# Output-weight low parts on the Vector engine, and one weight load moved behind the loads of b22

## The chip, the cores and the metric

The kernel runs on one core of a Trainium2 chip. Its engines work in parallel, each through its own queue in order: TensorE (PE in the profile; its weight loads are PEld), the Vector engine (DVE), the Scalar engine (ACT), GpSimd (POOL), and SyncE (SP), which here only issues DMA transfers. A wait at the head of a queue holds up everything behind it on that engine. The metric is the device time of one execution in microseconds; lower is better.

## What is computed

One layer of an encoder block on x (1, 1024, 1024) in float32, cut to what matters here:

```python
h = layer_norm(x, ln_in_g, ln_in_b)
proj = h @ w_in[l]
att = dilated_attention(aq, ak, av, slopes)
rec = hgrn2(hq, hf_fwd, hf_bwd, hi, hg, lower_bounds[:, l], hgrn_norm_g[l])
merged = sigmoid(ga) * (att @ w_att_up[l]) + sigmoid(gh) * (rec @ w_hgrn_up[l])
h = layer_norm(DEEPNORM_ALPHA * h + merged @ w_o[l], ln1_g[l], ln1_b[l])
gate, up = split(h @ w_ffn_in[l], 2, axis=-1)
h = layer_norm(DEEPNORM_ALPHA * h + (silu(gate) * up) @ w_ffn_out[l], ln2_g[l], ln2_b[l])
```

The change touches the line with `w_o` and the opening of the line with `w_ffn_in`. `w_ffn_in` is (1024, 5632); gate and up are 2816 columns each, worked on in 22 blocks of 128.

## The kernel before

**Precision.** Every matmul operand is split into a high part (a cast to float32r, on ACT, L205) and a low part (source minus high part, L209). `split` puts the low part on POOL unless `eng_lo="dve"` is given. A product is three matmuls per 128 rows: high by high (L255), low by high and high by low (L256, L257, in the order of the operands).

**Phase 2, output product.** The merged activations are transposed in `m0` and `m1`. `wo` has two halves of 512 columns, each a high and a low tile of 128 x 8 x 512. A half is made from four chunks of 128 columns by `wo_chunk`: a 512 KB load on SP into one of two `wraw` buffers (L1164), a cast on ACT and a subtraction on POOL, each over 1024 elements per partition. Chunks 0 to 3 are made during the recurrence's up-projection; chunks 4 to 7 after the pools of that stage are closed, since the second half lies in their memory. The order of TensorE then is: token block 0 with half 0, token block 1 with half 0, token block 0 with half 1, and from there both halves in turn. `half` evacuates a PSUM bank on DVE (L1263); `rest` takes statistics, normalises, transposes (L285) and hands the blocks for the feed-forward on.

**The feed-forward's opening.** The feed-forward input product is a Winograd form: seven products of half-size blocks per f (a pair of gate and up blocks of 128 columns). Their right-hand sides are b11, b21, t1, t2, which stay in SBUF, and b22, t3, t4, which `h1_blocks` stores to the scratch tensors `td[0]`, `td[1]`, `td[2]` (L1308) and `ffn_in` loads again in two pieces each as `t_raw` (L1465), with the high part on ACT and the low part on DVE. `ffn_raws` loads the two weight blocks of an f as `f_raw`, 512 KB each (L1403). The groups for f = 0, 1, 2 are begun early, with their products 1 and 2; then come products 5 and 6 (t1, t2), then 3 and 7 (b22, t3), then 4 (t4). The loads for f = 3 are the first that `ffn_in`'s own loop asks for; each takes the buffer of f = 0.

**What sets the order.** The program is written in one order; a planner then orders each engine's instructions by readiness and priority in a simulated timeline. `add_manual_dep` with a NoSync class adds an edge to that order without a semaphore. `ordered` chains instructions by such edges; `behind` ties one instruction to the last evacuation noted by `left`.

Of the kernel before, what the change touches and what calls it, by code (L numbers as in the profile page):

```python
# [79 lines left out]
class Block:  # L80
# [143 lines left out]
    def left(self, ins):  # L224
        self.gone = ins.ins.name

    def behind(self, ins):

        if self.gone is not None:
            self.tc.add_manual_dep(ins.ins, self.gone, mybir.DependencyInfo(  # L230
                mybir.DependencyClass.NoSync, mybir.DependencyReason.DATA), reason="order behind an evacuation")

    def queued(self, dst, src):
# [923 lines left out]
        for z in (resp, xpool, wspool, blkpool):  # L1157
            z.__exit__(None, None, None)

    def wo_chunk(self, hl, c):  # L1160
        nc, wp = self.nc, self.wp
        hi, lo = hl
        raw = self.wraw.tile([128, KT, 128], F32, name="w_raw", tag="wraw", bufs=2)
        nc.sync.dma_start(raw, self.wo[:, 128 * c:128 * c + 128].rearrange("(k p) c -> p k c", p=128))  # L1164
        s = slice(128 * (c % 4), 128 * (c % 4) + 128)
        self.split(hi[:, :, s], lo[:, :, s], raw)

    def phase2(self):
        nc = self.nc
        gc, bc = self.col["g1"], self.col["b1"]  # L1170
        with ExitStack() as es:
# [31 lines left out]
            wo = [[mp.tile([128, KT, HALF], F32R, name=f"wo0{n}") for n in ("hi", "lo")]]  # L1203
# [17 lines left out]
            wop = es.enter_context(self.pool("wop"))  # L1221
            wo.append([wop.tile([128, KT, HALF], F32R, name=f"wo1{n}") for n in ("hi", "lo")])
            for c in range(4, 8):
                self.wo_chunk(wo[1], c)
            yp = es.enter_context(self.pool("yp"))
            raws = []

# [13 lines left out]
            for t in range(8):  # L1241
                ms = []
                for k0 in (0, 4):
                    mh, ml = self.granules()
                    tk = slice(128 * (t % 4), 128 * (t % 4) + 128)
                    if t < 4:
                        for k in (0, 2):
                            self.split(mh[:, k:k + 2, :], ml[:, k:k + 2, :], m0[(k0 + k) // 2][:, :, tk],
                                       eng_lo="dve" if t == 0 and k0 else "pool")
# [146 lines left out]
        yield  # L1396
        out(1, 0, product(4, 1, False), None)

    def ffn_raws(self, f, pool=None, tag="fraw", bufs=4):
        out = []  # L1400
        for c in (128 * f, D_FF + 128 * f):
            r = (pool or self.rawp).tile([128, KT, 128], F32, name="f_raw", tag=tag, bufs=bufs)
            self.nc.sync.dma_start(r, self.wfi[:, c:c + 128].rearrange("(k p) c -> p k c", p=128))  # L1403
            out.append(r)
        return out

    def ffn_in(self):

        nc = self.nc
        with ExitStack() as es:  # L1410
# [9 lines left out]
            def evac_of(f):  # L1420
                c = acts[f] = fp.tile([128, T], F32, name="fc", tag="fc", bufs=4)
                th = fp.tile([128, T], F32, name="fth", tag="fth", bufs=2)

                def evac(i, l, ps, add):
                    s = slice(HALF * l, HALF * (l + 1))
                    if i == 0:
                        nc.vector.tensor_add(c[:, s], add, ps)
                        nc.scalar.activation(th[:, s], c[:, s], AF.Tanh, scale=0.5)
                        nc.vector.scalar_tensor_tensor(th[:, s], th[:, s], 1.0, c[:, s], op0=OP.add, op1=OP.mult)
                        return  # L1430
                    u = ps
                    if add is not None:
                        u = add
                        nc.vector.tensor_add(u, u, ps)
                    nc.vector.scalar_tensor_tensor(c[:, s], th[:, s], 0.5, u, op0=OP.mult, op1=OP.mult)

                    if l == 0 or f % 2:
                        nc.sync.dma_start(self.gd[4 if l else 1 + f % 2][:, f // 2], c[:, s])

                return evac  # L1440

            def sums(f):

                a11, a21, a12, a22 = (acts[f - 1 + i][:, HALF * l:HALF * (l + 1)] for i in range(2) for l in range(2))
                t = fp.tile([128, T], F32, name="fs", tag="fgl", bufs=2)
                s4 = fp.tile([128, T], F32, name="fs4", tag="fgh", bufs=2)[:, 0:HALF]
                s1, s2 = (t[:, HALF * i:HALF * (i + 1)] for i in range(2))
                nc.vector.tensor_add(s1, a21, a22)
                nc.vector.tensor_sub(a21, a11, a21)
                nc.vector.tensor_sub(s2, s1, a11)  # L1450
                nc.vector.tensor_sub(s4, a12, s2)
                for p, z in ((5, s1), (6, s2), (7, a21), (3, s4)):
                    nc.sync.dma_start(self.gd[p][:, f // 2], z)

            def vecs(v):
                t = self.abp.tile([128, D], F32, name="ab", tag="ab", bufs=2)
                nc.scalar.dma_start(t, bass.AP(tensor=v.tensor, offset=v.offset, ap=[[0, 128], [1, D]]))
                ab.append(t)

            self.first_evac = [evac_of(f) for f in range(3)]  # L1460
            for i, n in enumerate(("b22", "t3", "t4")):
                for k in (0, 2):
                    tag = "fgh" if k else "fgl"
                    r = fp.tile([128, 2, HALF], F32, name="t_raw", tag=tag, bufs=2)
                    nc.sync.dma_start(r, self.td[i][:, k:k + 2, :])  # L1465
                    hi, lo = self.xb[n]
                    self.split(hi[:, k:k + 2, :], lo[:, k:k + 2, :], r, eng_lo="dve")
            ab = []
# [4 lines left out]
            for f in range(2, NF):  # L1473
                if f > 2:
                    grp = self.wino_project(nxt, evac_of(f))
                next(grp)
                if f + 1 < NF:
                    nxt = self.ffn_raws(f + 1)
                next(held, None)
                if f % 2 == 0:  # L1480
                    sums(f - 1)
                next(grp)
                held = grp
                if f == 3:
                    for v in self.ln["1"]:
                        vecs(v)
                if 5 <= f < 21 and f % 2:
                    t = f // 2 - 2
                    n = fp.tile([128, D], F32, name="res", tag="fc", bufs=4)
                    nc.sync.dma_start(n, self.n1_d[t])  # L1490
                    nc.vector.scalar_tensor_tensor(n, n, ALPHA, ab[0], op0=OP.mult, op1=OP.mult)
                    nc.vector.scalar_tensor_tensor(n, ab[1], ALPHA, n, op0=OP.mult, op1=OP.add)
                    nc.scalar.dma_start(self.ahs_d[t], n)
            self.first_rows = []
            for f in range(6):
                p, tag, n = (self.rawp, "fraw", 4) if f < 4 else (self.abp, "ab", 2)
                r = p.tile([128, D], F32, name="w_rows", tag=tag, bufs=n)
# [239 lines left out]
```

## Time and profile before

| | us |
|---|---|
| median of 3 runs | 2134.19 |
| lowest and highest run | 2123.66, 2137.27 |
| profiled execution | 2131.49 |
| its span, first to last instruction | 2129.7 |

| engine | busy us in the profiled execution |
|---|---|
| TensorE matmul | 2029.0 |
| DVE | 1392.7 |
| POOL | 1077.5 |
| ACT | 919.7 |

A row of the timeline has start, length, engine, line, operation, output and inputs, shapes and count; in brackets stands the idle time of that engine before the row and what ended it. A row of the waits view has the waiting instruction, what released it, the total in us, the number of waits and the longest. SPq is SP's queue of DMA issues; its rows span from the first issue to the last of a run of equal ones.

### The profile page before, as it was taken

The numbers are of one execution on the slowest core, as the hardware profiler recorded it, in microseconds if no ns is written. First come the engines' busy times: TensorE is split into PE (matmuls) and PEld (weight loads), VectorE is DVE, ScalarE is ACT, GpSimd is POOL, SyncE is SP. The second block draws the span as 40 slices with busy tenths as digits, with TensorE's granted clock in tenths as the row PEclk, the third lists the DMA queues.
The fourth block names the chain that finished last, engine by engine and source line by source line (L and its number), as shares of the span: only waits on it lengthen the run. The fifth ranks groups of instructions, "written<-read, shape, count | busy, mean of one in ns | idle before, by whom it ended". The sixth has DMA issues, their size and how long they took to land.

```text
span 2129.7 us, 30900 instructions
## 1 busy us (share of the span) xinstructions
PE 2029.0 (95%) x10941; PEld 1674.6 (79%) x10941; DVE 1392.7 (65%) x2228; ACT 919.7 (43%) x1864; POOL 1077.5 (51%) x882
## 2 busy tenths in 40 slices
PE   4799999999999999999999899999999999999998
PEld 3678787788878788887888688878788888887876
DVE  7667746777459753788536712337867677767778
ACT  6544455434544435543355432135433333343542
POOL 3466653567536664465644754443656566630012
PEclk9899999999999999999999999999999999999999
DMA  5342442435424343333444755244434344348423
GB/s 202 109 133 95 147 155 73 144 118 167 130 92 141 135 146 125 124 129 109 146 130 142 283 188 164 89 139 139 154 109 153 129 144 134 117 160 291 158 89 124
DMA packets 273885, 301.10 MB, mean 141 GB/s; under 512 B 14081, under 2 KB 205378, under 8 KB 273730
## 3 DMA queue, kind: packets, MB, share of 16 engines
q1 hardware_dynamic: 266272, 273.73, 39.7%
q10 hardware_dynamic: 7458, 25.40, 3.0%
q8 instruction: 86, 1.41, 0.3%
q14 instruction: 69, 0.57, 0.1%
HBM read 200.25 MB, written 98.83 MB: 140 GB/s over the span
## 4 chain that ended last, share of the span: by engine, by line
PE 77%; DVE 12%; issue 5%; POOL 3%; DMA 2%; ACT 2%; SPq 0%; ACTq 0%; DVEq 0%; POOLq 0%
PE pj L255 17%; PE pj L256 17%; PE pj L257 16%; PE sd L256 6%; PE sd L255 6%; PE sd L257 6%; PE sd L1049 2%; POOL w_lo L209 1%; DVE qd L964 1%; DVE qd L967 1%; PE sd L998 1%; DVE p L849 1%; PE sd L863 1%; DVE fb L953 1%; ACT p L827 1%
## 5 line engine op out<-in xcount | busy, mean ns | idle before, releaser
L209 POOL TENSOR_TENSOR w_lo<-wa,w_hi 128x512 fp32r<-128x512 f32 x276 | 377.4, 1374 | 297.9 <-ACT w_hi L205 274.0
L205 ACT CAST w_hi<-wa 128x512 fp32r<-128x512 f32 x276 | 170.4, 619 | 245.8 <-PE pj L256 159.5
L209 POOL TENSOR_TENSOR w_lo<-wsum,w_hi 128x512 fp32r<-128x512 f32 x88 | 129.0, 1474 | 113.0 <-PE sd L257 60.4
L200 POOL TENSOR_TENSOR mv<-mv,mhalf 128x1 f32<-128x1 f32 x24 | 15.5, 647 | 228.6 <-DVE mv L199 225.5
L209 POOL TENSOR_TENSOR w_lo<-f_raw,w_hi 128x512 fp32r<-128x512 f32 x66 | 102.1, 1555 | 55.4 <-ACT w_hi L205 54.2
L255 PE MATMUL pj<-xt1hi,w_hi 128*128 128x512 f32 x260 | 103.9, 400 | 16.3 <-ACT xt1hi L205 10.7
L205 ACT CAST w_hi<-wsum 128x512 fp32r<-128x512 f32 x88 | 54.7, 621 | 124.6 <-PE sd L256 114.4
L255 PE MATMUL pj<-xb22hi,w_hi 128*128 128x512 f32 x260 | 102.6, 394 | 1.1 <-ACT wkeep L511 1.1
L256 PE MATMUL pj<-xt1lo,w_hi 128*128 128x512 f32 x260 | 102.3, 393 | 0.0
L257 PE MATMUL pj<-xt1hi,w_lo 128*128 128x512 f32 x260 | 102.0, 392 | 0.0
L256 PE MATMUL pj<-xb22lo,w_hi 128*128 128x512 f32 x260 | 101.5, 390 | 0.0
L257 PE MATMUL pj<-xb22hi,w_lo 128*128 128x512 f32 x260 | 101.3, 390 | 0.0
L209 POOL TENSOR_TENSOR w_lo<-ws,w_hi 128x512 fp32r<-128x512 f32 x46 | 63.0, 1373 | 69.2 <-ACT w_hi L205 63.3
L205 ACT CAST gwsum<-a_raw 128x512 fp32r<-128x512 f32 (+1 forms) x78 | 47.8, 616 | 102.9 <-PE pj L256 48.0
L511 ACT COPY wkeep<-pj 128x512 f32<-128x512 f32 x138 | 80.1, 582 | 22.1 <-DVE evh L430 10.1
L403 DVE TENSOR_TENSOR evh<-wkeep,pj 128x512 f32<-128x512 f32 x66 | 57.5, 879 | 48.5 <-PE pj L257 35.2
L209 DVE TENSOR_TENSOR gwkeep<-a_raw,gwsum 128x512 fp32r<-128x512 f32 (+1 forms) x78 | 57.7, 739 | 43.1 <-ACT gwsum L205 40.2
L489 POOL TENSOR_TENSOR wa<-wa,wa 128x512 f32<-128x512 f32 x46 | 67.6, 1480 | 35.6 <-DVE ws L488 27.6
L414 DVE TENSOR_TENSOR evh<-wkeep,pj 128x512 f32<-128x512 f32 x48 | 32.6, 681 | 80.7 <-PE pj L257 65.5
L255 PE MATMUL pj<-xt4hi,w_hi 128*128 128x512 f32 x192 | 77.8, 406 | 5.6 <-DVE evh L403 5.6
L257 PE MATMUL pj<-xt2hi,w_lo 128*128 128x512 f32 x192 | 76.1, 397 | 4.9 <-POOL w_lo L209 4.9
L255 PE MATMUL pj<-xb11hi,w_hi 128*128 128x512 f32 x192 | 77.3, 404 | 2.6 <-DVE evh L414 1.4
(406 smaller groups left out, 6587.1 us busy)
## 6 DMA issues: line engine op xcount, KB each, us to landing
wa<-in_w_in_dram SPq DMA_DIRECT2D x184, 256.0 KB, 3.1
f_raw<-in_w_ffn_in_dram SPq DMA_DIRECT2D x44, 512.0 KB, 4.2
a_raw<-gd SPq DMA_DIRECT2D x30, 512.0 KB, 3.5
gd<-fc SPq DMA_DIRECT2D x44, 256.0 KB, 2.0
gd<-fs SPq DMA_DIRECT2D x33, 256.0 KB, 2.1
tg<-evh SPq DMA_DIRECT2D x32, 256.0 KB, 3.5
tg<-tg SPq DMA_DIRECT2D x16, 512.0 KB, 3.7
y<-ahs SPq DMA_DIRECT2D x16, 512.0 KB, 5.5
```

The costliest lines, as they stand in the source:

```text
L205: nc.scalar.copy(hi, src)
L209: ins = e.tensor_sub(lo, src, hi.bitcast(F32))
L255: nc.tensor.matmul(ps, whi, xhi, start=first, stop=False, **kw)
L256: nc.tensor.matmul(ps, whi, xlo, start=False, stop=False, **kw)
L257: nc.tensor.matmul(ps, wlo, xhi, start=False, stop=last, **kw)
L403: self.left(nc.vector.tensor_tensor(o, self.order_src(add, g, kind), s, OP.add))
L414: self.left(nc.vector.tensor_add(t, add, ps))
L489: nc.gpsimd.tensor_sub(a["a21"], a["a11"], a["a21"])
L511: nc.scalar.copy(t, ps)
L827: nc.scalar.activation(z, z, AF.Exp, bias=N0[p, hd, tt:tt + 1], scale=QSCALE, accum_out=L0[p, hd, tt:tt + 1])
L849: nc.vector.tensor_scalar(z, z, W0[p, hd, tt:tt + 1], None, op0=OP.mult)
L1049: nc.tensor.matmul(po[:, jj, :], l, r, start=(n == 0), stop=(n == len(terms) - 1))
```

## The change

`wo_chunk` gets an argument for the engine of the low part, and chunks 4 to 7 pass "dve". `behind` may be given the instruction to stand behind; `ffn_raws` may pass one on; `ffn_in` keeps the name of the last of b22's two loads, and the loads for f = 3 (made in the loop's step f = 2) are ordered behind it.

```diff
-    def behind(self, ins):
-
-        if self.gone is not None:
-            self.tc.add_manual_dep(ins.ins, self.gone, mybir.DependencyInfo(
+    def behind(self, ins, last=None):
+
+        last = last or self.gone
+        if last is not None:
+            self.tc.add_manual_dep(ins.ins, last, mybir.DependencyInfo(
...
-    def wo_chunk(self, hl, c):
+    def wo_chunk(self, hl, c, by="pool"):
...
-        self.split(hi[:, :, s], lo[:, :, s], raw)
+        self.split(hi[:, :, s], lo[:, :, s], raw, eng_lo=by)
...
             for c in range(4, 8):
-                self.wo_chunk(wo[1], c)
+                self.wo_chunk(wo[1], c, "dve")
...
-    def ffn_raws(self, f, pool=None, tag="fraw", bufs=4):
+    def ffn_raws(self, f, pool=None, tag="fraw", bufs=4, after=None):
...
-            self.nc.sync.dma_start(r, self.wfi[:, c:c + 128].rearrange("(k p) c -> p k c", p=128))
+            ins = self.nc.sync.dma_start(r, self.wfi[:, c:c + 128].rearrange("(k p) c -> p k c", p=128))
+            if after:
+                self.behind(ins, after)
...
-                    nc.sync.dma_start(r, self.td[i][:, k:k + 2, :])
+                    ins = nc.sync.dma_start(r, self.td[i][:, k:k + 2, :])
+                    if i == 0:
+                        b22_load = ins.ins.name
...
-                    nxt = self.ffn_raws(f + 1)
+                    nxt = self.ffn_raws(f + 1, after=b22_load if f == 2 else None)
```

## The prediction, made before the change was run

> **What bounds the kernel now.** I read the page's first part, then the windows view with the span cut into stages, then the waits of TensorE after 1370 us, and last the timeline, engine by engine, around the two places those waits name.
>
> ```profile
> PE 2029.0 (95%) x10941; PEld 1674.6 (79%) x10941; DVE 1392.7 (65%) x2228; ACT 919.7 (43%) x1864; POOL 1077.5 (51%) x882
> ...
> 1376.00:1475.00 99.00, 96.13 (x446) 79.46 (x445) 48.22 (x98) 43.12 (x79) 44.44 (x38) 0.98 0.45 148
> 1475.00:1522.00 47.00, 42.23 (x176) 33.23 (x175) 40.50 (x44) 23.11 (x39) 27.00 (x19) 0.93 0.48 149
> 1522.00:1895.00 373.00, 373.00 (x1647) 308.60 (x1646) 268.75 (x255) 138.08 (x238) 234.27 (x157) 1.00 0.40 134
> ```
>
> The columns of the last three rows are the stretch, its length, then busy time and count of PE, PEld, DVE, ACT and POOL, the granted clock, the DMA share and GB/s. TensorE is the bound: 95% of the span. In the 373 us from 1522 it never stops (373.00 busy, 373 / 1647 = 0.226 us per matmul), so what is won ahead of 1522 is not absorbed there. The changed code lies in the first two stages, which is where TensorE does stop:
>
> ```profile
> PE sd L255 <- ACT xb22hi L205: 4.2, 1, 4.2
> PE pj L256 <- POOL wo1lo L209: 1.7, 1, 1.7
> PE pj L255 <- ACT wo1hi L205: 1.2, 1, 1.2
> ```
>
> The lower two are one place (the second half of the output weights), the upper one the other (b22). Each part of the change aims at one of them.
>
> **First part: low parts of output-weight chunks 4 to 7 on DVE.** What TensorE loses there:
>
> ```profile
> 1386.74 0.39 PE L257 MATMUL pj<-wo0hi,w_lo 128*128 128x512 f32 x1
> 1388.31 0.73 PE L255 MATMUL pj<-wo1hi,w_hi 128*128 128x512 f32 x2 [1.18 <-ACT wo1hi L205]
> 1390.74 0.80 PE L256 MATMUL pj<-wo1lo,w_hi 128*128 128x512 f32 x1 [1.69 <-POOL wo1lo L209]
> ...
> 1393.79 0.39 PE L257 MATMUL pj<-wo1hi,w_lo 128*128 128x512 f32 x1
> ...
> 1390.00:1391.00 1.00, 0.26 (x1) 0.26 (x2) 0.00 (x0) 0.00 (x0) 0.68 (x1) 0.62 1.10 332
> 1393.00:1394.00 1.00, 1.00 (x4) 0.81 (x3) 0.00 (x0) 0.00 (x0) 0.00 (x0) 0.67 0.68 203
> ```
>
> The next matmul was due at 1386.74 + 0.23 = 1386.97. Between it and 1393.79 nine start (two at 1388.31, then seven from 1390.74 on), worth 9 x 0.226 = 2.0 us. The place therefore costs 6.8 - 2.0 = 4.8 us: some 3.4 of waiting and 1.4 of slow clock, since the granted clock falls in 1390 to 1391 (0.62) and is back in 1393 to 1394 (0.67).
>
> The chain behind it:
>
> ```profile
> 1376.74 2.00 ACT L205 CAST wo1hi<-w_raw 128x1024 fp32r<-128x1024 f32 x2
> 1387.21 1.04 ACT L205 CAST wo1hi<-w_raw 128x1024 fp32r<-128x1024 f32 x1 [1.42 <-DMA w_raw<-in_w_o_dram]
> 1378.45 4.75 POOL L209 TENSOR_TENSOR wo1lo<-w_raw,wo1hi 128x1024 fp32r<-128x1024 f32 x2
> 1385.87 4.81 POOL L209 TENSOR_TENSOR wo1lo<-w_raw,wo1hi 128x1024 fp32r<-128x1024 f32 x2 [2.67 <-ACT wo1hi L205]
> 1380.87 2.75 SPq L1164 DMA_DIRECT2D w_raw<-in_w_o_dram  x2
> w_raw<-in_w_o_dram SPq DMA_DIRECT2D x2, 512.0 KB, 3.9
> 1377.01 0.88 DVE L1210 TENSOR_TENSOR mT<-mT,tg 128x512 f32<-128x512 f32 x1
> 1382.45 0.69 DVE L191 BATCH_NORM_STATS2 bn<-y 128x6 f32<-128x512 f32 x1
> 1387.17 0.69 DVE L1263 SCALAR_TENSOR_TENSOR y<-pj,y 128x512 f32<-128x512 f32 x1 [4.02 <-PE pj L257]
> L209 DVE TENSOR_TENSOR xt3lo<-t_raw,xt3hi 128x1024 fp32r<-128x1024 f32 x2 | 2.4, 1210 | 0.0
> ```
>
> There are two raw buffers. Chunks 4 and 5 lie in them; POOL needs 2.4 us for each low part, and only when one is done may SP load chunk 6 (1380.87) and chunk 7 (about 1383.2). A load lands 3.9 us later, ACT takes 1.04, POOL 2.4 again, and TensorE needs all four chunks.
>
> After the change four POOL subtractions of 2.4 us go (9.6 us) and four DVE ones of the same shape come. The row for that shape on DVE with POOL idle is xt3lo: 1.21 each, 4.8 us in all. DVE is free from 1377.01 + 0.88 = 1377.89, so chunk 4 is done at 1379.1, chunk 5 (its high part is ready at 1378.74) at 1380.3. The two loads leave then: 1.8 and 2.9 us earlier. Chunk 7 lands at 1380.3 + 3.9 = 1384.2, or some 1385.2 if it shares the engines with chunk 6 (my allowance). ACT: 1386.2; DVE: 1387.4. The first two matmuls need the high part only, 1386.97 + 2 x 0.226 = 1387.4. So the wait just closes, no clock falls, and the gain is the whole 4.8 us. The cover for the DVE work is its own idle time: 4.02 us before the evacuation at 1387.17. Who waits behind a DVE that stands at chunk 6 or 7 is the evacuation L1263 and its statistics; TensorE takes nothing of them before the transposes of that row block, 19 us later (the chain of waits, start and length), so that costs nothing.
>
> ```profile
> 1406.23 0.87 PE sd L285 x8
> ```
>
> Upper end for the subtraction:
>
> ```profile
> 1511.10 2.30 DVE L209 TENSOR_TENSOR xb22lo<-t_raw,xb22hi 128x1024 fp32r<-128x1024 f32 x1
> 1508.66 3.66 POOL L209 TENSOR_TENSOR w_lo<-wsum,w_hi 128x512 fp32r<-128x512 f32 x2 [3.79 <-ACT w_hi L205]
> ```
>
> This one began while POOL worked until 1508.66 + 3.66 = 1512.32, and took 2.30. I take 1.21, the nearest row, since POOL has nothing left after its activation splits at 1378.45; 2.30 is kept for a rival. The Trainium skill (SBUF — State Buffer, "SBUF: two separate sides") states a rule against this part: a DVE operation with two SBUF inputs and a GpSimd operation that reads SBUF exclude each other, the later one blocks entirely. The trace agrees: 1.22 us to POOL's end plus 1.21 makes 2.43, against 2.30. By it chunk 4 would start at 1378.45 instead of 1377.9 and the sum would be 0.5 us smaller.
>
> **Second part: the weight block behind b22.** What is lost, and the chain:
>
> ```profile
> 1503.49 0.39 PE L257 MATMUL pj<-xt2hi,w_lo 128*128 128x512 f32 x1
> 1508.12 1.31 PE L255 MATMUL sd<-xb22hi,w_hi 128*128 128x512 f32 x2 [4.24 <-ACT xb22hi L205]
> 1509.38 0.79 PE L256 MATMUL sd<-xb22lo,w_hi 128*128 128x512 f32 x1
> ...
> 1513.27 0.40 PE L257 MATMUL sd<-xb22hi,w_lo 128*128 128x512 f32 x1
> ...
> 1492.76 6.82 SPq L1308 DMA_DIRECT2D td<-tsum  x2
> 1499.67 0.58 SPq L1403 DMA_DIRECT2D f_raw<-in_w_ffn_in_dram  x1
> 1500.36 2.26 SPq L1465 DMA_DIRECT2D t_raw<-td  x4
> ...
> 1517.46 8.35 SPq L1403 DMA_DIRECT2D f_raw<-in_w_ffn_in_dram  x2
> ...
> 1507.02 1.04 ACT L205 CAST xb22hi<-t_raw 128x1024 fp32r<-128x1024 f32 x1 [4.71 <-DMA t_raw<-td]
> 1503.66 1.75 DVE L1344 TENSOR_TENSOR wsum<-f_raw 128x512 f32<-128x512 f32 x1
> 1508.09 1.23 DVE L209 TENSOR_TENSOR xb22lo<-t_raw,xb22hi 128x1024 fp32r<-128x1024 f32 x1 [2.68 <-ACT xb22hi L205]
> ```
>
> From 1503.49 + 0.23 = 1503.72 to 1513.27 eleven matmuls start (two at 1508.12, nine from 1509.38 on), worth 2.5 us, and take 9.55: 7.0 lost. On SP stand, in this order: the stores of t3 and t4 (done issuing at 1492.76 + 6.82 = 1499.58), one f_raw load at 1499.67 (the gate block of f = 3), then b22's two loads and t3's two. b22's first load is issued at 1500.36 and lands only at 1507.02, 6.7 us later, behind the 512 KB of the f_raw block. The change puts that f_raw behind b22's second load; the other f_raw block of f = 3 comes at 1517.46 and is behind it either way.
>
> Nothing is added or removed; one issue of 0.6 us and its transfer change place. b22's first load is issued at 1499.67. Its landing time alone: the same shape from the other scratch tensor,
>
> ```profile
> a_raw<-gd SPq DMA_DIRECT2D x30, 512.0 KB, 3.5
> ```
>
> gives 1503.2; with the t4 store still ahead of it I take 1503.7. ACT is done at 1504.8, and TensorE starts its first two matmuls 3.3 us earlier. The low part needs DVE, which is busy until 1503.66 + 1.75 = 1505.41, then takes 1.23. So the shift is capped by DVE: exactly the 2.68 us for which it stood idle before xb22lo. DVE is nearly full in this stage (40.50 of 47 us, those 2.68 among the rest), so the whole opening moves by 2.7 us and no more. Bounds: 0 if t3's loads come late in b22's place (the f_raw block now runs between them), and 4.5 (7.0 less the 1.1 us to 1504.8 and the 1.4 between two high-part matmuls and a low part at 1506.6) if another order of DVE's queue lifts the cap. I take 2.7.
>
> The moved block has no early reader; the first is
>
> ```profile
> 1528.90 1.78 DVE L1344 TENSOR_TENSOR wsum<-wsum,f_raw 128x512 f32<-128x512 f32 x1
> ```
>
> 29 us after its issue, so its delay of a few us costs nothing.
>
> **Sum.** 4.8 + 2.7 = 7.5 us. The profiled execution took 2131.49 us (its span 2129.7 and 1.8 around it): 2124.0. It lies 2.7 below the median of the runs shown (2134.19), so on the median: 2126.7.
>
> **Rivals.**
>
> *Half of the first part.* DVE puts the evacuation at 1387.17 and its statistics (0.69 each) ahead of chunk 7, or the subtractions cost 2.30. Then the last low part is done near 1389.8, only 0.9 ahead of 1390.74: gain 0.9 + 2.7 = 3.6, time 2130.6. For it: chunk 7 and that evacuation fall due within 1 us of each other. Against: DVE has 4 us of idle time there.
>
> *The b22 part gives nothing.* t3 or the t4 store sets the pace of the opening: gain 4.8, time 2129.4. For it: the same 2.5 MB pass the queue. Against: the second f_raw and t4 are not needed until much later. This is also the case in which the change doesn't do what it says, if another load takes the freed place ahead of b22.
>
> *Slower.* The first two low parts stand in DVE's queue behind the first evacuation, which waits for TensorE and ends with its statistics at 1382.45 + 0.69 = 1383.1 (POOL had done one by 1380.8). Then 1384.3 and 1385.5 for them, loads land at 1388.2 and 1390, ACT 1391.0, DVE 1392.3: 1.5 us later than 1390.74, and a second dip of the clock costs 1.4 again. That is +2.9 where -4.8 was expected. It decides as soon as that evacuation is ahead of chunk 4 and the b22 part brings less than 2.9; with that part at 0.4, +2.5: 2136.7. Against it: chunk 4 is ready 3.8 us before the evacuation.
>
> **How the numbers follow.** Forecast 0.50, half of the first part 0.15, b22 nothing 0.17, slower 0.13, something unnamed 0.05. The likeliest case gives 2126.7. Its own range is 2125 to 2129 (second part 4.5 to 0). The runs of before spread from 2123.66 to 2137.27 about 2134.19, so the low end is 2126.7 - 10.5 = 2116; the high end takes in the slower rival, 2138. One per cent is 21 us, about what a measurement of this kernel can tell from no change. No case reaches it; I leave 0.03 to faster and 0.04 to slower by over 1%.
>
> **What would show it.** Right: TensorE's waits on wo1hi and wo1lo gone or under 0.5 us and no dip of the clock near 1390; wo1lo on DVE at 1.2 us; chunk 7 loaded near 1380.3; the f_raw of f = 3 after b22's second load; the wait on xb22hi at 1 to 2 us with DVE's idle time before xb22lo gone. Wrong: a TensorE wait on a DVE wo1lo of 2 us or more, a new wait on xt3hi or xt3lo, or new waits in the 373 us that have none now; the last would mean that the order of the feed-forward's instructions changed as a whole.

## The result, and the profile after

| | before | after |
|---|---|---|
| median of 18 runs each, us | 2131.06 | 2124.05 |
| lowest and highest run | 2122.23, 2137.27 | 2116.25, 2128.63 |
| profiled execution | 2131.49 | 2124.65 |
| its span | 2129.7 | 2122.8 |

The ratio after to before is 0.997, with a 95% interval of 0.9958 to 0.9982: a small gain, but a sure one. TensorE's order of instructions is the same in both kernels. DVE's order has four subtractions more and POOL's four fewer, and on SP the weight block moved. With the weight block the planner also exchanged neighbours in the opening, at two places on DVE (the second xt4lo now stands behind both multiplications of L1432 and directly ahead of wkeep) and at three on ACT; the kernel with the first part alone has none of these exchanges. TensorE's waits of the kernel after, from 1490 to 1525 us, the stretch of the second place (the view has none for the first place, 1370 to 1420):

```profile
PE sd L256 <- ACT xb22hi L205: 1.8, 1, 1.8
PE sd L257 <- DVE xt3lo L209: 0.7, 1, 0.7
PE sd L256 <- DVE wkeep L1437: 0.6, 1, 0.6
PE sd L257 <- DVE xb22lo L209: 0.2, 1, 0.2
```

The two waits on the output weights are gone, and the wait on b22 fell from 4.2 to 1.8 us, but three small new ones stand behind it (xt3lo, wkeep, xb22lo), all on DVE. The windows view of the kernel after, same stretches and columns as in the prediction:

```profile
1376.00:1475.00 99.00, 98.88 (x465) 82.16 (x464) 56.61 (x106) 44.35 (x82) 36.85 (x37) 1.00 0.47 152
1475.00:1522.00 47.00, 43.10 (x185) 33.35 (x184) 42.87 (x45) 23.50 (x39) 30.16 (x19) 1.00 0.47 146
1522.00:1895.00 373.00, 373.00 (x1647) 308.96 (x1646) 266.99 (x256) 138.52 (x238) 229.69 (x154) 1.00 0.40 134
```

The granted clock is 1.00 in the first two stretches (0.98 and 0.93 before): both dips are gone in this execution. The 373 us still have no idle time, so what was won ahead of them was kept.

The first place in the timeline of the kernel after:

```profile
1379.02 2.88 DVE L209 TENSOR_TENSOR wo1lo<-w_raw,wo1hi 128x1024 fp32r<-128x1024 f32 x2
1380.80 1.52 SPq L1165 DMA_DIRECT2D w_raw<-in_w_o_dram  x2
...
1386.54 1.05 ACT L205 CAST wo1hi<-w_raw 128x1024 fp32r<-128x1024 f32 x1 [0.62 <-DMA w_raw<-in_w_o_dram]
...
1387.62 1.23 DVE L209 TENSOR_TENSOR wo1lo<-w_raw,wo1hi 128x1024 fp32r<-128x1024 f32 x1 [0.44 <-ACT wo1hi L205]
...
1388.17 0.61 PE L256 MATMUL pj<-wo1hi,w_hi 128*128 128x512 f32 x2
1388.76 0.68 DVE L1264 SCALAR_TENSOR_TENSOR y<-pj,y 128x512 f32<-128x512 f32 x1
1388.90 0.51 PE L257 MATMUL pj<-wo1lo,w_hi 128*128 128x512 f32 x1
...
1390.64 0.40 PE L258 MATMUL pj<-wo1hi,w_lo 128*128 128x512 f32 x1
```

TensorE comes to the second half at 1388.17 and goes on at 1388.90; nine matmuls start from 1388.17 to before 1390.64, worth 2.04 us of the 2.47, so 0.4 us is lost here where 4.8 was. Chunk 7's low part is done at 1388.85, and the evacuation (L1264) runs behind it.

The second place:

```profile
1496.59 1.95 SPq L1468 DMA_DIRECT2D t_raw<-td  x4
1498.66 3.45 SPq L1404 DMA_DIRECT2D f_raw<-in_w_ffn_in_dram  x2
...
1500.35 0.39 PE L258 MATMUL pj<-xt2hi,w_lo 128*128 128x512 f32 x1
1500.49 1.75 DVE L1345 TENSOR_TENSOR wsum<-f_raw 128x512 f32<-128x512 f32 x1
1501.46 1.04 ACT L205 CAST xb22hi<-t_raw 128x1024 fp32r<-128x1024 f32 x1 [2.32 <-DMA t_raw<-td]
1502.54 1.23 DVE L209 TENSOR_TENSOR xb22lo<-t_raw,xb22hi 128x1024 fp32r<-128x1024 f32 x1 [0.29 <-ACT xb22hi L205]
1502.56 1.02 PE L256 MATMUL sd<-xb22hi,w_hi 128*128 128x512 f32 x2 [1.82 <-ACT xb22hi L205]
1503.82 0.50 PE L257 MATMUL sd<-xb22lo,w_hi 128*128 128x512 f32 x1 [0.24 <-DVE xb22lo L209]
...
1515.20 1.28 DVE L1432 SCALAR_TENSOR_TENSOR fth<-fth,fc 128x512 f32<-128x512 f32 x2
```

The four loads of b22 and t3 now go out ahead of both f_raw blocks. b22 is there 4.9 us after its issue (6.7 before), and DVE's idle time ahead of xb22lo fell from 2.68 to 0.29 us.

The clock had a share in the second place too. The windows of the kernel before:

```profile
1506.00:1507.00 1.00, 0.00 (x0) 0.00 (x0) 0.00 (x0) 0.00 (x0) 0.00 (x0) 0.65 0.97 393
...
1508.00:1509.00 1.00, 0.89 (x2) 0.57 (x2) 0.91 (x1) 1.00 (x4) 0.34 (x1) 0.50 1.01 406
...
1513.00:1514.00 1.00, 1.00 (x6) 0.82 (x5) 1.00 (x2) 0.00 (x0) 0.00 (x0) 0.94 0.10 29
```

A mean of 0.65 is 0.7 us at 0.50, one of 0.94 is 0.1, so the clock was halved from 1506.3 to 1513.1, 6.8 us. Of these, 5.0 lie behind the start of b22's product at 1508.12, and 2.5 of the 7.0 us lost there are theirs. The kernel after has no such dip here.

To compare executions, each profile is cut at four TensorE starts that every kernel has: the first output product, the first matmul of t1 (product 5), and the first matmul that writes pj in t4's product (product 4 of the second f). "Head" is all before the first, "wo" lies between the first two and holds the first place, "opening" between the second and the third and holds the second place, "tail" is the rest of the span. All in us, worked out from the timelines:

```
kernel            span     head      wo      opening   tail
before            2129.7   1376.09   116.02  37.95     599.64
before_again      2131.6   1379.34   116.79  38.06     597.41
after             2122.8   1377.29   111.67  35.54     598.30
after_again       2121.5   1374.64   111.95  36.73     598.18
only_wo           2119.5   1371.65   111.66  38.55     597.64
wo_45             2125.0   1374.42   115.41  38.23     596.94
wo_67             2128.0   1373.53   115.79  38.31     600.37
only_b22          2125.5   1374.69   116.15  36.72     597.94
only_b22_again    2122.6   1371.74   116.23  36.82     597.81
t4_act            2127.2   1376.65   111.82  39.10     599.63
fth_behind        2123.6   1374.72   111.65  40.48     596.75
b22_first         2125.0   1380.86   112.03  34.07     598.04
b22_first_again   2117.4   1373.32   112.38  34.06     597.64
f3_late           2117.7   1373.07   112.14  35.87     596.62
```

In the first pair the 6.9 us of span are 4.35 in wo, 2.41 in the opening and 1.34 in the tail, less 1.20 lost in the head. Every engine's order is the same in all of these kernels up to the end of the head, and yet the head lies anywhere from 1371.7 to 1380.9. The spans of two single executions can therefore not be set against each other at this size; the two stages in which the change lies can, since they repeat far better.

The clock differs in the opening as well. It is halved there for 6.8 us in the five profiles with the loads as before and in `t4_act`, for 3.4 us in `after_again`, both of `only_b22`, `fth_behind` and `f3_late`, and not at all in the first profile of the kernel after and both of `b22_first`.

### The profile page after: what moved, and what is told of

Read it like the earlier page. It is cut to its first block, busy times and chain, and to the rows that moved or that the text cites. A ratio compares the mean times of both kernels' runs of the same rounds, so it can differ in the third digit from the quotient of the medians.

```text
span 2122.8 us, 30900 instructions
## 1 busy us (share of the span) xinstructions
PE 2026.3 (95%) x10941; PEld 1673.6 (79%) x10941; DVE 1399.0 (66%) x2232; ACT 919.5 (43%) x1864; POOL 1068.7 (50%) x878
## 4 chain that ended last, share of the span: by engine, by line
PE 54%; DVE 7%; DMA 2%; issue 2%; POOL 2%; ACT 1%; SPq 0%; ACTq 0%; DVEq 0%; POOLq 0%
PE pj L258 11%; PE pj L257 11%; PE pj L256 11%; PE sd L257 6%; PE sd L256 6%; PE sd L258 6%; POOL w_lo L209 1%; PE sd L1050 1%; ACT p L828 1%; DVE qd L965 1%; PE sd L999 0%; DVE fb L954 0%; DVE wa L494 0%; DVE p L850 0%; DMA binb<-in_ln_in_b_dram 0%
## 5 line engine op out<-in xcount | busy, mean ns | idle before, releaser
L490 POOL TENSOR_TENSOR wa<-wa,wa 128x512 f32<-128x512 f32 x46 | 68.0, 1490 | 36.8 <-DVE ws L489 33.5
L256 PE MATMUL pj<-xt2hi,w_hi 128*128 128x512 f32 x192 | 77.4, 404 | 1.8 <-ACT xt2hi L205 1.8
```

The source lines that it names most:

```text
L256: nc.tensor.matmul(ps, whi, xhi, start=first, stop=False, **kw)
L490: nc.gpsimd.tensor_sub(a["a21"], a["a11"], a["a21"])
```

## The experiments

The labels are those of the table. The kernels of one group ran on one chip, beside the kernel before.

### The two parts apart, and the first part in halves

`only_wo` is the change without its second part, `only_b22` without its first. `wo_45` and `wo_67` take the first part alone, for two of its four chunks.

```diff
 # only_wo, wo_45, wo_67
-                    nxt = self.ffn_raws(f + 1, after=b22_load if f == 2 else None)
+                    nxt = self.ffn_raws(f + 1, after=None)
 # only_b22
-                self.wo_chunk(wo[1], c, "dve")
+                self.wo_chunk(wo[1], c)
 # wo_45
+                self.wo_chunk(wo[1], c, "dve" if c < 6 else "pool")
 # wo_67
+                self.wo_chunk(wo[1], c, "pool" if c < 6 else "dve")
```

> The first part alone (low parts of chunks 4 to 7 on DVE; the weight load of f = 3 stays ahead of b22). Theory: the two parts are separate places with separate prices, so this one gives what the stage with the output weights gave in the changed kernel, 4.4 us: TensorE has no wait on wo1hi or wo1lo over 0.3 us, the clock stays at 1.00 from 1376 to 1400 us, and the later wait on xb22hi stays at 4.2 us with its clock dip. Span about 2125, ratio about 0.998. Rival (the two places share one cost, for instance the phase of the clock window): the gain alone is 2 us or less, or 6 and more.

> The second part alone (low parts stay on POOL; the load of f = 3 behind b22). Theory: 2.4 us, the wait on xb22hi falls from 4.2 to 1.8 us and DVE's idle time before the first xb22lo from 2.68 to about 0.3; the waits on wo1hi (1.2) and wo1lo (1.7) stay, with the clock dip near 1390. Span about 2127, ratio about 0.999. Rival (the wait also gets a full clock back, which DVE does not cap): 4 us.

> Only chunks 4 and 5 have their low parts on DVE, 6 and 7 on POOL; the b22 part is left out. Theory: the gain has two halves, the raw buffers freed sooner (loads of 6 and 7 leave some 1.3 and 2.2 us earlier) and the last subtractions shorter. Here the loads leave early, but POOL then needs 2 x 2.4 us for chunks 6 and 7, so TensorE's wait on wo1lo is still about 2 us: gain 1 to 1.5 us, and up to 1.4 more if the clock does not dip. Rival A (the buffers' release is all): 4.4 us, no wait left. Rival B (the last subtractions are all): 0.

> Only chunks 6 and 7 have their low parts on DVE, 4 and 5 on POOL; the b22 part is left out. Theory: the loads leave as late as before (the second near 1383.2), chunk 7's high part is ready near 1388.2 and its low part 1.2 us later instead of 2.4: the wait on wo1hi stays at 1.2, that on wo1lo falls from 1.7 to about 0.5: gain about 1.2 us, and up to 1.4 more if the clock does not dip. Rival A (the buffers' release is all): 0. Rival B (the last subtractions are all): 4.4 us.

Measured against the kernel before (median 2129.29): `only_wo` 2124.34, ratio 0.9973 (0.9963 to 0.9984); `only_b22` 2128.90, 0.999 (0.9978 to 1.0002); `wo_45` 2127.22, 0.9994 (0.9984 to 1.0005); `wo_67` 2127.73, 0.9993 (0.9983 to 1.0003).

The first part stands alone: wo falls from 116.02 to 111.66, and the opening does not gain (38.55). The second part alone brings 1.2 us in the opening, half of what the first profile of the kernel after showed; its own ratio does not tell it from no change.

The halves bring little: 0.6 and 0.2 us in wo against the first profile of the kernel before, 0.9 and 0.5 against the mean of the four profiles without the first part (116.3). Some 1 to 1.5 us was expected of each, and the waits did shrink about as expected. So neither the earlier release of the buffers nor the shorter last subtractions is the gain by itself. Waits of `wo_67`:

```profile
PE pj L256 <- ACT wo1hi L205: 1.5, 1, 1.5
PE pj L257 <- DVE wo1lo L209: 0.6, 1, 0.6
```

That is 2.1 us against 2.9 before, and `wo_45` waits 2.28. Part of it was handed back by the clock. The windows of `wo_45` around its wait:

```profile
1388.00:1389.00 1.00, 0.79 (x3) 0.70 (x4) 0.00 (x0) 0.00 (x0) 0.16 (x1) 0.91 1.01 303
1389.00:1390.00 1.00, 1.00 (x3) 0.73 (x3) 0.00 (x0) 0.00 (x0) 0.00 (x0) 0.50 0.51 149
1390.00:1391.00 1.00, 1.00 (x4) 0.78 (x3) 0.00 (x0) 0.00 (x0) 0.00 (x0) 0.50 1.00 297
1391.00:1392.00 1.00, 1.00 (x4) 0.81 (x3) 0.00 (x0) 0.00 (x0) 0.00 (x0) 0.50 0.42 120
1392.00:1393.00 1.00, 1.00 (x5) 0.78 (x5) 0.00 (x0) 0.55 (x2) 0.07 (x1) 0.88 0.00 0
```

From 1388.8 to 1392.2 (0.91 and 0.88 are the ends of it) the granted clock is 0.50, and a matmul starts every 0.43 us instead of every 0.23. In the kernel before, part of such a stretch fell into the wait itself (0.26 us of TensorE work in the window from 1390); here the wait is over sooner and the whole stretch runs under load. Counted as in the prediction, `wo_45` loses 4.2 us at the place (13 matmuls start between 1385.31 and 1392.42), some 2.5 by standing and 1.7 by the clock, and `wo_67` the same; before it was 4.8 (3.3 and 1.5). So while the wait only shrinks, the clock keeps its 1.5 and takes 0.2 more. Only a wait that closes takes the dip along: all eight profiles with the whole first part have at most 0.6 us of waiting at the place and no dip near 1390, all six others stand there for 2 us or more and have it.

### Does DVE cap the second part?

The prediction's cap says that b22 may land as early as it likes, since DVE is busy. `t4_act` lets b22 land earlier still: t4's last store, which stands ahead of b22's loads on SP, is issued from ACT. `b22_first` does the same and also lifts the cap: two multiplications of the evacuations of f = 0 and 1 (L1432) are ordered behind b22's second low part on DVE. `f3_late` tests that the moved block has no early reader, and puts it behind t4's last load. `before_again` shows what two profiles of one kernel differ by.

```diff
 # t4_act, b22_first
-            nc.sync.dma_start(self.td[i][:, :, c], v)
+            (nc.scalar if t == 7 and i == 2 else nc.sync).dma_start(self.td[i][:, :, c], v)
 # b22_first (split returns its last instruction)
-                        nc.vector.scalar_tensor_tensor(th[:, s], th[:, s], 1.0, c[:, s], op0=OP.add, op1=OP.mult)
+                        o = nc.vector.scalar_tensor_tensor(th[:, s], th[:, s], 1.0, c[:, s], op0=OP.add, op1=OP.mult)
+                        if f < 2 and l == 0:
+                            self.behind(o, self.b22_low)
...
-                    self.split(hi[:, k:k + 2, :], lo[:, k:k + 2, :], r, eng_lo="dve")
+                    low = self.split(hi[:, k:k + 2, :], lo[:, k:k + 2, :], r, eng_lo="dve")
+                    if i == 0:
+                        self.b22_low = low.ins.name
 # f3_late
-                    if i == 0:
+                    if i == 2:
                         b22_load = ins.ins.name
```

> Both parts, and the last store of t4 (token block 7) leaves on ACT's queue instead of SP's, so that b22's loads no longer stand behind a store that waits for DVE: they can leave some 6 us earlier. TensorE's order is that of the changed kernel, DVE's has one pair swapped. Theory (DVE caps the opening: it is busy without a pause until the first xb22lo): the wait on xb22hi (1.8 us) goes, a wait on xb22lo of about 2 us comes in its place, DVE's idle time before xb22lo (0.29) goes; the opening, from the first matmul with xt1 to the product with xt4 that took 35.54 us in the changed kernel and 37.95 before, is shorter by 0.3 us at most. Rival (the landing of b22 is the cap): shorter by 1.8 to 2.8 us, no wait on b22 left.

> As t4_act, and the two operations of the first evacuations on DVE that stand ahead of xb22lo (2.4 us in the changed kernel) are ordered behind the second xb22lo. Theory (DVE's order caps the opening): xb22lo starts up to 2.4 us earlier and TensorE waits for b22 under 1 us in all; the opening takes 33.5 to 34.5 us, ratio to before about 0.996. Rival (DVE's total work caps it, whatever the order: it is 40 to 43 us of the 47 us stage): the wait moves to xt3lo, xt4lo or wkeep and the opening stays at 35 us or more.

> Both parts, but the loads of f = 3 stand behind the last load of t4 instead of the last of b22, some 5 us later still. Theory: the block is first read by DVE 20 us and more after its issue, so the opening stays at 35.5 us to within 0.5 and there is no wait on f_raw or on s2 (wsum). Rival (the moved block is late for someone): a new wait of DVE on the load of f_raw and an opening longer by 2 us or more.

> The kernel before, unchanged, for a second profile. Theory: of the stretches compared, the one from the first output product to the first matmul with xt1 (116.02 us) and the opening (37.95 us) repeat within 0.5 us, apart from the phase of the clock window, while the 1376 us ahead of them and the 600 us behind them differ by 1 to 4 us from run to run. Rival: all four repeat within 0.5 us, so that the 1.3 us which the changed kernel gained behind the opening belong to the change.

Measured against the kernel before (median 2131.15): `t4_act` 2125.52, ratio 0.9975 (0.9964 to 0.9987); `b22_first` 2122.22, 0.9954 (0.9937 to 0.9971); `f3_late`, one run, 2119.46; `before_again`, one run, 2133.41.

`t4_act`, timeline:

```profile
1498.19 1.06 ACT L205 CAST xb22hi<-t_raw 128x1024 fp32r<-128x1024 f32 x1
1499.47 1.78 DVE L1345 TENSOR_TENSOR wsum<-f_raw 128x512 f32<-128x512 f32 x1
1500.13 0.61 PE L256 MATMUL sd<-xb22hi,w_hi 128*128 128x512 f32 x2
1501.18 1.75 DVE L1432 SCALAR_TENSOR_TENSOR fth<-fth,fc 128x512 f32<-128x512 f32 x1
1502.86 2.29 DVE L209 TENSOR_TENSOR xb22lo<-t_raw,xb22hi 128x1024 fp32r<-128x1024 f32 x1
...
1505.19 0.80 PE L257 MATMUL sd<-xb22lo,w_hi 128*128 128x512 f32 x1 [4.45 <-DVE xb22lo L209]
```

b22's high part is ready before TensorE comes to it, and TensorE does not wait for it at all; then it waits 4.45 us for the low part, because DVE is at other work until 1502.86. The cap holds: the earlier landing moved the wait to DVE and did not shorten the opening. It even lengthened it to 39.10, which was not expected: DVE stood idle 0.96 us before this work, so that xb22lo began 14.4 us after the start of product 5 instead of 13.6 in the kernel after; the subtraction itself took 2.29 us; and the clock was halved for 6.8 us. This execution was the longest of the 12.

`b22_first`, timeline:

```profile
1503.88 2.32 DVE L209 TENSOR_TENSOR xb22lo<-t_raw,xb22hi 128x1024 fp32r<-128x1024 f32 x1
1504.53 0.61 PE L257 MATMUL sd<-xb22hi,w_hi 128*128 128x512 f32 x2
1506.25 0.50 PE L258 MATMUL sd<-xb22lo,w_hi 128*128 128x512 f32 x1 [1.11 <-DVE xb22lo L209]
...
1510.21 1.28 DVE L1433 SCALAR_TENSOR_TENSOR fth<-fth,fc 128x512 f32<-128x512 f32 x2
```

With those multiplications out of the way TensorE waits 1.1 us for the first low part and 0.8 for the second (under 1 in all was expected), and the opening is 34.07, 3.9 shorter than before. DVE's order is not the only difference, though: the planner gave TensorE another order as well. Eight matmuls that write pj with t2 now stand ahead of the first ones with t4, which in the kernel after wait 0.6 us for wkeep and here for nothing. As long as TensorE's order is the same, for the first 86 matmuls of the opening, `b22_first` leads the kernel after by 0.4 us; at the end of the opening it leads by 1.5. How much of that is due to DVE's order and how much to TensorE's no run separates.

`f3_late` has an opening of 35.87, as good as that of the kernel after (35.54): the f = 3 blocks go out 18.8 us after the start of product 5 instead of 9.7, and TensorE waits for nothing of theirs. `before_again` repeats the opening within 0.1, and wo only within 0.8, where 0.5 had been expected; its tail is 2.2 shorter than in the first profile of the same kernel. So the 1.34 us in the tail of the first pair are within the scatter.

### Repeats, and the order of DVE alone

`after_again`, `b22_first_again` and `only_b22_again` are the same kernels once more, to see what of the second part repeats. `fth_behind` is `b22_first` with t4's store back on SP: the order of DVE's queue without the earlier landing.

> The changed kernel once more, beside b22_first on the same chip. Theory: ratio to before 0.997 again; in the profile the stretch from the first output product to xt1 repeats at 111.7 us within 0.3, with no wait over 0.5 us on wo1, and the opening lies between 35 and 37 us, according to how many DVE operations meet a POOL subtraction (0.7 or 1.8 us, 1.2 or 2.3 us for the same operation). Rival: the opening repeats to 0.2 us, and the 36.72 us of only_b22 come from the first part's absence.

> b22_first once more on the same chip as after_again. Theory: the opening is again 1 to 2 us shorter than that of after_again, 34 to 35 us, and the ratio to before some 0.0005 to 0.001 below that of after_again. Rival: the difference was scatter; the same ratio and the same opening within 0.3 us.

> The second part alone once more, one look. Theory: the opening varies with the meetings of DVE and POOL, so it lies anywhere from 35 to 37 us, and the wait on xb22hi is 1.8 to 2.1 us again. Rival: 36.7 us to within 0.2.

> Both parts and only the order of DVE from b22_first (the two operations of the first evacuations behind the second xb22lo), with t4's last store back on SP, so that b22 lands as late as in the changed kernel. Theory: now the landing is the cap; DVE stands idle 2 us and more before xb22lo and does the 2.4 us of work after it, so the opening is no shorter than in the changed kernel, 35.5 to 38 us, with the wait on xb22hi at 1.8 us still there. Rival (the order of DVE alone gives b22_first's gain): 34 us.

Measured against the kernel before (median 2128.54): `after_again` 2122.04, ratio 0.9979 (0.9967 to 0.999); `b22_first_again` 2121.36, 0.9971 (0.9956 to 0.9985); `only_b22_again`, one run, 2124.38; `fth_behind`, one run, 2125.43.

The opening of `b22_first` repeats to 0.01. That of the kernel after doesn't: 36.73 instead of 35.54, and `only_b22` stays at 36.8. So 35.54 was the lucky one. What differs is seen in the waits of `only_b22`,

```profile
PE sd L256 <- ACT xb22hi L205: 1.9, 1, 1.9
...
PE sd L256 <- DVE wkeep L1437: 1.5, 1, 1.5
```

and in the timeline of `after_again`:

```profile
1511.83 3.48 DVE L1432 SCALAR_TENSOR_TENSOR fth<-fth,fc 128x512 f32<-128x512 f32 x2
1515.23 2.31 DVE L209 TENSOR_TENSOR xt4lo<-t_raw,xt4hi 128x1024 fp32r<-128x1024 f32 x1
1517.46 0.68 DVE L1437 TENSOR_TENSOR wkeep<-wkeep,sd 128x512 f32<-128x512 f32 x1
```

The same pair of DVE multiplications took 1.28 us in the first profile and 3.48 here, and both times in `only_b22`. In the first profile POOL had next to nothing to do during them; here it worked all the time. TensorE pays for it with a longer wait on wkeep (1.2 to 1.6 us against 0.6). These three executions also have one dip of the clock in the opening, which the first profile lacks. In `after_again` TensorE comes to that wait 0.6 us later than in the first profile, but DVE, at work without a pause from 1510.05 on, ends it 1.2 us later, and behind it both need the same 5.1 us. So the 1.2 us come by way of DVE; how far the dip had made DVE's own inputs late stays open. `f3_late` has the dip and the slow pair and still reaches 35.87: there the second xt4lo stands ahead of the pair, and TensorE does not wait for wkeep.

`fth_behind` makes the opening worse than was expected (35.5 to 38), 40.48: the wait on xb22hi stays at 1.8, the multiplications now stand in front of t3's low part, and TensorE waits 2.2 us for xt3lo and 2.1 for wkeep. The order pays only together with the earlier landing.

`b22_first` has the shortest opening, 1.5 and 2.7 us shorter than those of the kernel after. That its total is shorter is not shown: beside each other on one chip the two have 0.9971 and 0.9979, and the intervals overlap.

## Why the prediction was right, point by point

**The time.** Predicted 2126.7, measured 2124.05; predicted for the profiled execution 2124.0, measured 2124.65. The predicted change was -7.5; the medians differ by 7.0 and, in the repeat, 6.5. The measured median lies just below the 2125 to 2129 given for the likeliest case, because the median of the kernel before came down with it, from 2134.19 in 3 runs to 2131.06 in 18. That the profiled execution was met within 0.7 us is luck: its head alone ranges over 9 us.

**The first part: mechanism right, the term 0.4 too large.** Predicted -4.8. Over all profiles that hold the whole first part, eight, wo has a mean of 111.9; over the four that hold none of it, 116.3: -4.4. Step by step, with the 1.2 us added by which TensorE was later here: chunk 7's data were predicted for 1386.4 and came at 1386.5, its low part for 1388.6 and came at 1388.85; 0.4 us were lost where none was predicted. The step that was off is the price of the first subtraction. The lines view of the kernel after, with minimum, median and maximum in ns:

```profile
L209 DVE TENSOR_TENSOR wo1lo<-w_raw,wo1hi x4: 1209/1226/1747, 1379.0 to 1387.6; 128x1024 fp32r<-128x1024 f32 x4
```

Three took 1.2 us as predicted, the first 1.75: POOL was still at its activation splits when it began. That repeats: the first took 1.75 us in all nine profiles with chunk 4 on DVE. The prediction had reckoned this way and then set it aside: the Trainium skill (SBUF — State Buffer, "SBUF: two separate sides") has whichever of the two engines comes second blocked for the whole of the other's instruction, which gave 0.5 us less, thus 4.3. The run sides with the Trainium skill: 4.35 in the first pair, 4.4 in the mean. That this half microsecond is all that was missing is likely but not shown, since wo itself repeats only within 0.8.

**The rivals to the first part.** DVE put the first evacuation behind chunks 4 and 5 and the second behind chunk 7, so neither the half nor the slower rival came about. The slower rival's danger was real in kind: `wo_45` and `wo_67` show that a chain which stays 2 us late keeps the dip of the clock, and gives part of its gain back to it.

**The second part: direction right, the term too large, and the clock left out.** Predicted -2.7, "exactly the 2.68 us" for which DVE stood idle. At the start of b22's product the working is the predicted one: DVE's idle time fell by 2.39, TensorE's wait by 2.42. It fell short of 2.68 because b22 took 4.9 us from issue to landing where 4.0 was assumed, so that the landing and its cast still ended last, 0.29 us behind DVE.

That the whole opening then gave 2.41 is partly luck. The prediction had DVE pace the stage to its end. In the kernel before, TensorE waits for nothing behind b22's start; what costs it time there is the halved clock (2.5 us). From b22's start to the end of the opening both kernels need 21.9 us, before with the dip and without a wait, after without the dip and with 1.5 us of waits on xb22lo, xt3lo and wkeep. These waits are DVE's, so it does pace the stage once b22 is earlier; but the agreement rests on a dip that went and waits that came, of about the same size, and the prediction has neither. A new wait on xt3lo it had even named as a sign of being wrong.

The cap also counted DVE's operations as having fixed lengths. They do not: part of what was won in idle time went into operations that now met POOL's. The four openings with the second part (35.54, 36.73, 36.72, 36.82) have a mean of 36.5, the five with the loads as before (before, `before_again`, `only_wo`, `wo_45`, `wo_67`) one of 38.2: -1.8, and -1.4 to -1.5 in three of the four. How these 1.8 divide between the wait, the clock and the exchanged neighbours on DVE and ACT is not shown. The rival by which the b22 part gives nothing is contradicted by the openings; the run times of `only_b22` alone could not tell. Of the bounds, 0 to 4.5, the upper is nearly reached by `b22_first` (3.9 below the kernel before), with another order of DVE's queue, as the text supposed, but of TensorE's too.

**The moved block.** That its delay costs nothing held, and `f3_late` shows more room. Two statements about the move were wrong, and the sum did not rest on them. More than one issue changed place, since the planner exchanged neighbours on DVE and ACT too. And the second block of f = 3 did not come at 1517.46 in the kernel before but between the loads of t3 and t4, at 1504.89: the change also put it, with the first, behind t3's loads and ahead of t4's.

**The sum.** 4.4 + 1.8 = 6.2, where 7.5 was predicted. Each part alone took 4.95 us (`only_wo`) and 0.4 (`only_b22`) off the median. The medians of both say 7.0 and 6.5, and the ratio's interval alone spans 3.8 to 9.0 us; the head and tail of a single profile scatter by more than either part.

## What to carry to other kernels

Where a wait and the clock dip behind it are one loss, count them together, and expect little from an edit that only shortens the wait: nearly the whole loss goes when the wait closes (4.4 us here), little of it when it shrinks by a quarter (0.2 to 0.9 us). In a stage that another engine comes to pace, expect no more from an earlier transfer than that engine's idle time, and less where its operations grow when they meet a third engine's. Where a planner sets the order, compare every engine's order before and after: moving one transfer exchanged neighbours on two other engines here. When the expected change is a third of a per cent, cut the profiles at fixed instructions and compare the stages: the stages here repeat to about a microsecond while the spans of one kernel do not.

## What the hardware did that was not expected

**A multiplication of 0.68 us can take 1.78.** The DVE operations of the opening that read two operands from SBUF come mostly in two lengths 1.1 us apart, 1.21 and 2.31 for 1024 elements, 0.68 and 1.78 for 512, so the difference does not grow with the operation's size. What counts is whether POOL was already at work when the operation began. From 1476 to 1535 us, in all 14 profiles together, every one of the 266 that began while POOL stood still was short, even where POOL began during it, and all 235 lengthened ones began during an operation of POOL; another 33 that began then were short. The 143 operations with an operand in PSUM were short whatever POOL did.

**A short gap can drop the clock, and need not.** The kernel after and `only_b22` wait almost equally long for b22 (1.82 and 1.85 us). The windows of `only_b22`, where TensorE goes on at 1504.47:

```profile
1504.00:1505.00 1.00, 0.51 (x2) 0.19 (x2) 0.68 (x2) 1.00 (x3) 0.00 (x0) 1.00 1.03 418
1505.00:1506.00 1.00, 1.00 (x2) 0.50 (x3) 0.68 (x1) 1.00 (x2) 0.98 (x1) 0.54 1.03 419
1506.00:1507.00 1.00, 1.00 (x3) 0.81 (x4) 0.15 (x1) 1.00 (x2) 0.82 (x1) 0.50 1.05 353
```

Its clock falls 0.6 us after the wait is over (0.54 is 0.92 us at 0.50), when TensorE is busy again; in the first profile of the kernel after it stays at 1.00 all through. `after_again` waits 1.87 us there and has the dip. The Trainium skill (TensorE: Matmul & The Clock Gate, "What's actually happening") tells of a window of about 3.4 us that runs free of the program. The lengths of the dips agree with it (3.4 us in `wo_45`, and twice that, 6.8, in the opening of the kernel before), and so does it that the same wait is punished in one execution and not in the other. Its condition, at least one such window of idleness, does not: in `only_b22` TensorE had stood for less than 2 us at a stretch.
